# Two-layer hybrid backbone on one core: attention with one score buffer, z projections spread over its units, scan matmuls grouped by shape

## The chip, the core and the metric

The kernel runs on one core of a Trainium2 chip. The metric is device time in microseconds (us) of one execution. Five engines work beside each other, each taking its own instructions in order: TensorE (PE, matmuls, its weight loads shown apart as PEld), VectorE (DVE), ScalarE (ACT), GpSimd (POOL) and SyncE (SP, which issues most DMAs). Matmuls write to PSUM, which has eight banks of 512 fp32 columns.

## The reference, cut to what matters

Two layers work on 512 latent tokens and 256 context tokens of width 1024. Each layer is one mixer: normalise and modulate, one combined input projection, three head groups side by side, an output projection with a residual.

```
p = split_projection(h @ w_in)          # r,k,v,lora,z | conv b,c,h,z | q,k,v,z of the attention
rwkv:  S = S*w + (S a) b^T + v k^T ;  y = S r        (both directions, context first, then latents)
attn:  s = q k^T ;  p_j = softmax(s_j)  (j = 0, 1) ;  o = (p_0 - lam * p_1) v
       out = rms_norm(o) * silu(z)
x = x + gate * rms_norm(concat(rwkv, conv, attn) @ w_out)
```

The attention has four heads, each with two score maps. Layer 0 yields latents and context, so it has six query blocks of 128 rows; layer 1 yields latents only, four blocks.

## The kernel before, in words

Each operand of the big matmuls is split into a high and a low fp32r part, and a projection is three matmuls for each of eight 128-row slices (hi*hi, hi*lo, lo*hi). One projection of one 128-wide channel group is a run of 24 matmuls of 512 columns for the latents (`pcl`) and, where the context is needed, 24 of 256 columns (`pcc`); `proj_ch` is a Python generator that issues one of them per step. Token-major projections are `ptl` and `ptc`.

The projections not needed at once wait in a queue of generators, `fq`. `fill(us)` issues matmuls from the queue until their nominal lengths (0.213 us for 512 columns) sum to `us`; such filler stands between dependent steps. A list scheduler then orders each engine's instructions by priority, which is the place in the program, and by its own picture of when inputs are ready. `keep_in_program_order` pins an instruction behind the one issued before it on its engine; `T.matmul(..., tail=True)` does that and also raises its priority, so that a group of matmuls stays together.

A layer goes through these stages. First come the projections that the scan needs. Then the scan (`rwkv_scan`) runs in three blocks of four steps. A step works on both directions: `ch<-zu,R` (R0, state times stage matrix), a copy `gs` on DVE, `ch<-gs,XT`, four copies `zu` that alternate between ACT and DVE, `ch<-zu,R` again (R1), and four DVE additions that make the next `zu`. Where output is wanted there are also `yps<-zu,rt` (called rt below) and `yps<-zu,R` (R2). Every one of these is 8 fp32 matmuls, 16 instructions in the trace, on a part of the array: R0, R1 and R2 on 128x64, XT and rt on 64x64, while the filler uses 128x128. `fill(F["a"])`, `fill(F["b"])` and `fill(F["c"])` stand between them. In block 0 of layer 1 no output is wanted. Then `rwkv_out` normalises and transposes the scan's output, with filler beside it, and `fill(1e9)` empties the queue.

The attention (`attention`) is a software pipeline over units, a unit being one head and one query block (in layer 0 the two context blocks form one unit): 20 units in layer 0, 16 in layer 1. For a unit, PE writes the scores of both maps (`sc`, 8 matmuls) to a PSUM buffer of three banks, DVE takes two maxima (`mx`), ACT two exponentials (`e<-sc`), each with a read of the accumulator, DVE and POOL combine the maps, PE transposes (`aT_mm`, tile `aTp`), ACT copies (`aT_cp`), PE multiplies by v (`av`) and ACT drains the result with a copy and a square (`drain`, tiles `O`, `osq`). At iteration x the pipeline works on the scores of unit x+3, the exponentials of x+2, the combination of x+1 and the rest of x. `lin["on"]` pins all PE work of this stage in program order, and `order` does so for the main ACT and DVE work. `finish(h)` normalises a head, transposes it (`oT`), multiplies by silu(z) and writes the result, split, into slice 4+h of `lat` and `ctx`, which are the projections' own inputs.

Before the change the z projections of the attention (`z_gate`, four channel groups) are filler of the `rwkv_out` stage, and q and k of heads 2 and 3 (`qk(2)`, `qk(3)`) are filler of the attention's first three iterations (16 and three times 6 nominal us), with the rest issued at x = 0. Then the filler's three PSUM banks are given up (`az_done`), and a second score buffer `pr1` takes them: from there on the scores alternate between two buffers. The units themselves have no filler.

Of the kernel before, what the change touches and what calls it, by code (L numbers as in the profile page):

```python
# [50 lines left out]
EB = (3,2)  # L51
ATB = 2
ORD = [(0,), (4, 5), (1,), (2,), (3,)]
# [10 lines left out]
FI2 = 3  # L64
FA = (16,6)
QV = (2,3)
# [10 lines left out]
WM = 2  # L77
ZB = 1
PA = 3
# [27 lines left out]
def build(tc, A):  # L107
# [19 lines left out]
    class T:  # L127
        @staticmethod
        def matmul(*a, tail=False, **k):
            if tail:  # L130
                with tc.high_priority(offset=400):
                    tc.keep_in_program_order(nc.tensor.matmul(*a, **k))  # L132
                return
            i = nc.tensor.matmul(*a, **k)  # L134
            if lin["on"] or lin.get("next"):
                tc.keep_in_program_order(i)
                lin["next"] = False

        @staticmethod
# [674 lines left out]
    def rwkv_scan(l, st, rw, lat, cx):  # L814
# [38 lines left out]
        for b in range(3):  # L853
# [37 lines left out]
            for p in range(4):  # L891
# [15 lines left out]
                for d in range(2):  # L907
                    for hp, h, hr in HH:
                        T.matmul(pv[d][hr, 0, hp, :], R[d][:, hp, h, 0, :], zu[d][:, hp, h, :], start=True, stop=True)
                if want_y:  # L910
                    for d in range(2):
                        py[d] = ps("y", "yps").rearrange("p (k a v) -> p k a v", k=4, a=2)
                        for hp, h, hr in HH:
                            T.matmul(py[d][hr, 0, hp, :], prepd[d][0][hr, hp, cc[d][1], :], zu[d][hr, hp, h, :],
                                     start=(hp == 0), stop=False, tile_position=(h * 64, h * 64), skip_group_check=True)
                for d in range(2):
                    gs[d] = rw.tile([P, 2, HD], F32, tag="gs", bufs=2, name="gs")
                    V.tensor_copy(gs[d], pv[d][:, 0])
                if not end:
# [19 lines left out]
                if not end:  # L939
                    for d in range(2):  # L940
                        nz[d] = new_zu(nb, d, np_)
                        for hp, h, hr in HH:
                            T.matmul(pv[d][hr, 0, hp, :], R[d][:, hp, h, 1, :], zu[d][:, hp, h, :], start=True, stop=True)
# [110 lines left out]

    def z_gate(l, cnt, dst, mul, lat, cx, fk=()):
        last = l == L - 1
        n = NL if last else NT
        for h in range(cnt):
            t = fst("zs")
# [10 lines left out]
    def attn_proj(l, lat, cx):  # L1070
# [82 lines left out]
    def attention(l, lat, cx, pool, az_done, hd0):  # L1153
# [85 lines left out]
        def aT_mm(u, i):  # L1239
            b0, b1 = ((0, 3), (3, 6))[i] if len(u["tt"]) == 1 else ((0, 2), (2, 4))[i]  # L1240
            pt = u["pt"] = ps("a", "aTp")
            for kt in range(b0, b1):
                T.transpose(pt[:, (kt - b0) * P:(kt - b0 + 1) * P], u["e", 0][:, kt * P:(kt + 1) * P], ident)

        def aT_cp(u, i):
            b0, b1 = ((0, 3), (3, 6))[i] if len(u["tt"]) == 1 else ((0, 2), (2, 4))[i]
            if AC >> i & 1:
                dv(V.tensor_copy(u["aT"][:, b0 * P:b1 * P], u["pt"][:, :(b1 - b0) * P]))
            else:
                ac(S.copy(u["aT"][:, b0 * P:b1 * P], u["pt"][:, :(b1 - b0) * P]))  # L1250

# [24 lines left out]
        def finish(h, O):  # L1276
# [42 lines left out]
        def at(i):  # L1319
            return us[i] if 0 <= i < len(us) else None  # L1320

        for x in range(-3, len(us)):
# [10 lines left out]
            if p:  # L1333
                drain(p)
            if u:
                aT_cp(u, 0)
            if c:
                coef(c)
                combine(c)
            if e and x < 0:  # L1340
                expo(e, 0)
                expo(e, 1)
                e = None
            if w:
                scores(w, 0)
            if e:
                expo(e, 0)
            if u:
                aT_mm(u, 1)
                aT_cp(u, 1)  # L1350
            if w:
                scores(w, 1)
                maxi(w, 0)
                maxi(w, 1)
                head_next(w)
            if e:
                expo(e, 1)
            if u:
                av(u)
            else:  # L1360
                fill(FA[1])
            if u and u["i"] == FI and u["h"]:
                fins.append(finish(u["h"] - 1, Os[u["h"] - 1]))
                next(fins[-1])
            if u and u["i"] == FI2 and u["h"]:
                next(fins[-1])
        drain(us[-1])
# [78 lines left out]
    for l in range(L):  # L1446
# [23 lines left out]
        with tc.tile_pool(name=f"yy{l}", bufs=1, reuse_waits="tile") as yy:  # L1470
            with tc.tile_pool(name=f"rw{l}", bufs=1, reuse_waits="tile") as rw:
# [12 lines left out]
                ap1, ap2, az = attn_proj(l, lat, cx)  # L1484
                fq[:] = must + [rwkv_v(l, lat, cx), z_gate(l, 2, zrd[l], 0.5, lat, cx), conv(l, lat, cx)] + ap1
                rwkv_scan(l, st, rw, lat, cx)
# [30 lines left out]
            with tc.tile_pool(name=f"at{l}", bufs=1, reuse_waits="tile") as at:  # L1517
# [17 lines left out]
                if not YE:  # L1535
                    wo = y_split()
                psum_end(f"q0{l}", f"q3{l}")
                psum(f"y{l}", dict(b=3))
# [159 lines left out]
```

## Time and profile before

| | us |
|---|---|
| runs: lowest, median, highest | 1171.63, 1181.82, 1189.62 |
| the profiled execution's own time | 1183.87 |
| its span in the trace | 1181.6 |
| PE busy | 1061.3 |
| DVE busy | 733.6 |
| ACT busy | 525.2 |

A row of the timeline gives the start, the length, the engine, the line, the operation with out<-in, and the count of merged instructions; in brackets the engine's idle time before it and who ended that. Starts are us from the span's start. PE rows overlap: matmuls are pipelined, so the distance between starts is what a matmul costs. Line L134 and L118 are the helpers that record matmuls and DVE work. The granted clock (PEclk) is 1.00 at 2.4 GHz and 0.50 at 1.2 GHz.

### The profile page before, as it was taken

What the parts mean: (1) busy time and instruction counts of PE and PEld (TensorE: products, weight loads), DVE (VectorE), ACT (ScalarE), POOL (GpSimd) and SP (SyncE); (2) the same over time, 40 slices, a digit from 0 to 9 for tenths busy, and PEclk for the clock granted to TensorE, in tenths of its full rate; (3) what the DMA queues carried; (4) which work ended last, traced back from release to release, by engine and by line L of the source; (5) the groups of instructions that cost most, each with busy time, mean ns of one, the idle gap of its engine ahead of it and who ended that gap; (6) DMA issues with size and microseconds to landing.
All of it is one profiled execution on the core that took longest, in us unless ns stands there. A gap on an engine that the chain in (4) does not pass through costs nothing.

```text
span 1181.6 us, 25468 instructions
## 1 busy us (share of the span) xinstructions
PE 1061.3 (90%) x9850; PEld 857.7 (73%) x9850; DVE 733.6 (62%) x1712; ACT 525.2 (44%) x1330; POOL 485.6 (41%) x508
## 2 busy tenths in 40 slices
PE   4899989989699999979899899989969989988797
PEld 1577968667578867868777776866757876777675
DVE  3430658588647243389947867776893813569945
ACT  4323563353353223368733664655334422338731
POOL 1211524425624513355532345254572443456532
PEclk9999999999899999999999999999999989999999
DMA  9473321212424346745052452232331334555143
GB/s 350 169 238 116 89 78 47 60 28 70 144 55 117 122 148 203 205 153 139 14 183 72 143 178 78 85 92 59 95 99 50 104 101 128 181 153 176 46 151 107
DMA packets 92088, 142.55 MB, mean 121 GB/s; under 512 B 28192, under 2 KB 36416, under 8 KB 91968
## 3 DMA queue, kind: packets, MB, share of 16 engines
q1 hardware_dynamic: 88512, 136.14, 37.3%
q10 hardware_dynamic: 3456, 4.80, 1.2%
q8 instruction: 77, 1.26, 0.5%
q14 instruction: 43, 0.35, 0.1%
HBM read 110.99 MB, written 25.71 MB: 116 GB/s over the span
## 4 chain that ended last, share of the span: by engine, by line
PE 50%; DVE 22%; ACT 7%; issue 5%; DMA 5%; POOL 4%; SPq 1%; ACTq 0%; DVEq 0%; POOLq 0%
PE pcl L134 16%; PE op L134 6%; PE ptl L134 5%; PE pcc L134 4%; PE ch L134 3%; DVE mx L118 3%; PE yps L134 3%; PE ptc L134 3%; DVE bk L118 2%; DMA mraw<-in_mod_w_dram 2%; DVE rs_t L118 1%; PE av L134 1%; DVE qkr L118 1%; PE s L134 1%; DVE e L118 1%
## 5 line engine op out<-in xcount | busy, mean ns | idle before, releaser
L260 POOL TENSOR_TENSOR wlo<-wraw,whi 128x512 fp32r<-128x512 f32 x134 | 180.3, 1349 | 317.8 <-ACT whi L257 278.1
L134 PE MATMUL pcl<-lat,whi 128*128 128x512 f32 (+1 forms) x928 | 301.4, 399 | 3.5 <-issue 1.8
L134 PEld LDWEIGHTS pcl<-lat,whi 128*128 128x128 f32 x928 | 170.3, 190 | 43.7 <-issue 8.8
L134 PE MATMUL pcl<-lat,wlo 128*128 128x512 f32 (+1 forms) x464 | 185.8, 400 | 3.8 <-POOL wlo L260 3.8
L257 ACT CAST whi<-wraw 128x512 fp32r<-128x512 f32 x144 | 88.4, 618 | 170.8 <-DMA wraw<-in_w_in_dram 44.2
L134 PE MATMUL pcc<-ctx,whi 128*128 128x256 f32 x576 | 109.6, 287 | 2.3 <-DVE ctx L118 1.7
L134 PEld LDWEIGHTS pcl<-lat,wlo 128*128 128x128 f32 x464 | 88.3, 190 | 27.2 <-POOL wlo L260 5.7
L134 PEld LDWEIGHTS pcc<-ctx,whi 128*128 128x128 f32 x576 | 92.2, 191 | 8.7 <-issue 2.6
L134 PE MATMUL pcc<-ctx,wlo 128*128 128x256 f32 x288 | 83.1, 289 | 2.0 <-DVE wlo L118 2.0
L134 PE MATMUL ptl<-whi,lat 128*128 128x256 f32 x384 | 83.4, 300 | 0.0
L1215 ACT ACTIVATE e<-sc,mx 128x768 f32<-128x768 f32 (+1 forms) x80 | 66.5, 834 | 20.7 <-DVE mx L118 15.4
L118 DVE TENSOR_REDUCE mx<-sc 128x1 f32<-128x768 f32 (+1 forms) x72 | 63.6, 918 | 15.8 <-PE sc L134 15.8
L134 PE MATMUL av<-vA,aT 128*128 128x128 f32 x416 | 60.1, 288 | 14.9 <-ACT aT L1250 14.7
L134 PEld LDWEIGHTS av<-vA,aT 128*128 128x128 f32 x416 | 54.9, 197 | 21.9 <-ACT aT L1250 18.8
L134 PEld LDWEIGHTS ptl<-whi,lat 128*128 128x128 f32 x384 | 65.4, 200 | 2.7 <-issue 0.7
L924 POOL TENSOR_TENSOR pz<-zu,pc 64x128 f32<-64x128 f32 x88 | 37.4, 425 | 60.6 <-DVE zu L118 55.8
L118 DVE TENSOR_TENSOR R<-s,cs 128x384 f32<-128x384 f32 (+1 forms) x96 | 47.0, 529 | 23.8 <-PE s L132 23.2
L134 PE MATMUL sc<-KH,QS 128*128 128x256 f32 (+1 forms) x144 | 52.7, 379 | 6.1 <-ACT qkr L1083 3.2
L134 PE MATMUL ptl<-wlo,lat 128*128 128x256 f32 x192 | 58.1, 302 | 0.0
L134 PEld LDWEIGHTS pcc<-ctx,wlo 128*128 128x128 f32 x288 | 55.0, 191 | 4.0 <-DVE wlo L118 2.2
L118 DVE TENSOR_TENSOR qkr<-qkr,qks 128x512 f32<-128x512 f32 (+2 forms) x24 | 25.5, 1063 | 34.0 <-POOL qkr L1090 26.3
L134 PE MATMUL sc<-KL,QS 128*128 128x256 f32 (+1 forms) x144 | 46.2, 342 | 0.0
(441 smaller groups left out, 2447.0 us busy)
## 6 DMA issues: line engine op xcount, KB each, us to landing
wraw<-in_w_in_dram SPq DMA_DIRECT2D x144, 256.0 KB, 2.6
mraw<-in_mod_w_dram SPq DMA_DIRECT2D x96, 256.0 KB, 4.5
KH<-qd SPq DMA_DIRECT2D x32, 192.0 KB, 3.7
oraw<-in_w_out_dram SPq DMA_DIRECT2D x20, 256.0 KB, 4.1
qd<-qks SPq DMA_DIRECT2D x12, 384.0 KB, 2.4
qd<-qkr SPq DMA_DIRECT2D x12, 384.0 KB, 2.5
qks<-qkr SPq DMA_DIRECT2D x64, 64.0 KB, 2.2
zu<-vd SPq DMA_DIRECT2D x96, 32.0 KB, 2.1
```

Of the source, the lines that this page charges most:

```text
L118: i = f(*a, **k)
L134: i = nc.tensor.matmul(*a, **k)
L257: S.copy(hi, raw)
L260: eng.tensor_tensor(out=lo, in0=raw, in1=hi.bitcast(F32), op=ALU.subtract)
L924: G.tensor_tensor(out=pz[d][hr], in0=zu[d][hr, :, h, :], in1=prepd[d][1][hr, :, cc[d][1]].unsqueeze(2).to_broadcast([64, 2, HD]), op=ALU.mult)
L1215: ac(S.activation(ej[:, c], pb[:, c], AF.Exp, bias=mx[:, i:i + 1], accum_out=den[:, u["h"] * 6 + tt, j:j + 1]))
```

## The change

In the scan, the rt matmuls are issued after `fill(F["a"])`, right ahead of XT, and a scheduling edge keeps them behind the last `gs` copy. Within each group all matmuls but the first get `tail`; XT is pinned behind rt, and R2 behind R1.

In the attention, `qk(2)` and `qk(3)` become filler of the `rwkv_out` stage, and the z projections, now one generator for each head, become filler of the attention: 4 nominal us at its start and 3 in each of the first three iterations, then 1.1 (layer 0) or 0.8 (layer 1) in each unit, half behind each group of transposes. The filler's PSUM banks stay in use to the end, so there is one score buffer. The order in an iteration is now: exponential of map 0, drain, exponential of map 1, transposes with filler, their copies, combination, all scores, maxima, `av`. Since `finish` overwrites `lat`, its last part for heads 0 and 1 is put off to head 3, after all z projections. `zT` gets three buffers, `aT` one.

```diff
-ATB = 2
+ATB = 1
-FA = (16,6)
+FA = (4,3)
+FU = (1.1,0.8)
-ZB = 1
+ZB = 3
@@ rwkv_scan
-                        T.matmul(pv[d][hr, 0, hp, :], R[d][:, hp, h, 0, :], zu[d][:, hp, h, :], start=True, stop=True)
-                if want_y:
-                    for d in range(2):
-                        py[d] = ps("y", "yps").rearrange("p (k a v) -> p k a v", k=4, a=2)
...
+                        T.matmul(pv[d][hr, 0, hp, :], R[d][:, hp, h, 0, :], zu[d][:, hp, h, :], start=True, stop=True,
+                                 tail=d + hp + h > 0)
...
                 fill(F["a"] if want_y else F["n"])
                 adv(AS)
                 lin["next"] = MG & 8
+                if want_y:
+                    for d in range(2):
+                        py[d] = ps("y", "yps").rearrange("p (k a v) -> p k a v", k=4, a=2)
+                        for hp, h, hr in HH:
+                            i = T.matmul(py[d][hr, 0, hp, :], prepd[d][0][hr, hp, cc[d][1], :], zu[d][hr, hp, h, :],
+                                     start=(hp == 0), stop=False, tile_position=(h * 64, h * 64), skip_group_check=True,
+                                     tail=d + hp + h > 0)
+                            if i is not None:
+                                tc.add_manual_dep(i.ins, cp.ins.name, mybir.DependencyInfo(
+                                    mybir.DependencyClass.NoSync, mybir.DependencyReason.DATA), reason="order")
...
-                                 start=True, stop=True)
+                                 start=True, stop=True, tail=want_y or d + hp + h > 0)
...
-                                     start=False, stop=True, skip_group_check=True)
+                                     start=False, stop=True, skip_group_check=True, tail=not end or d + hp + h > 0)
@@ attn_proj
+        chs(l, [x + h for h in (2, 3) for x in (I_Q, I_KA)])
         chs(l, range(I_AZ, I_AZ + 4))
-        chs(l, [x + h for h in (2, 3) for x in (I_Q, I_KA)])
-        return [qk(0), v(0), qk(1), v(1)], [z_gate(l, 4, zd[l], sgc, lat, cx, FK2)], [qk(2), qk(3)]
+        return ([qk(0), v(0), qk(1), v(1)], [qk(2, FK2), qk(3, FK2)],
+                [z_gate(l, (h,), zd[l], sgc, lat, cx, FK2) for h in range(4)])
@@ attention
+            if h < 2:
+                yield
...
+        fu = FU[l]
...
-            if x == FX:
-                fill(1e9)
-                az_done()
...
+            if e:
+                expo(e, 0)
+            if p:
+                drain(p)
+            if e:
+                expo(e, 1)
             if u:
                 aT_mm(u, 0)
...
+                fill(fu * 0.5)
+                aT_mm(u, 1)
+                fill(fu * 0.5)
                 aT_cp(u, 0)
+                aT_cp(u, 1)
+            else:
+                fill(FA[1])
             if c:
                 coef(c)
                 combine(c)
...
             if w:
                 scores(w, 0)
...
                 scores(w, 1)
                 maxi(w, 0)
                 maxi(w, 1)
...
+            if u and u["h"] == 3 and u["i"] < 2:
+                fill(1e9)
+                fin_next(u["i"])
+        az_done()
@@ build
             def az_done():
                 psum_end(f"f{l}")
-                psum(f"q3{l}", dict(pr1=1), "right")
-                cur["pr"] = ["pr1", "pr0"]
```

## Rows read from the trace of the kernel before

**Rows 1.** Busy time by stretch: length, busy of PE, PEld, DVE, ACT, POOL, granted clock, DMA share, GB/s

```profile
405.00:434.00 29.00, 29.00 (x338) 19.38 (x334) 11.18 (x38) 5.27 (x15) 8.48 (x13) 1.00 0.36 101
541.00:593.00 52.00, 44.20 (x319) 38.80 (x319) 46.34 (x107) 41.83 (x136) 29.15 (x32) 1.00 0.25 63
```

**Rows 2.** Timeline of PE, one scan step of layer 0, from one XT to the next

```profile
405.50 0.68 PE L134 MATMUL ch<-gs,XT 64*64 64x64 f32 x16
...
408.96 0.69 PE L134 MATMUL ch<-zu,R 128*64 128x64 f32 x16
409.48 0.40 PE L134 MATMUL yps<-zu,R 128*64 128x64 f32 x6
...
413.16 0.33 PE L134 MATMUL ch<-gs,XT 64*64 64x64 f32 x4
```

**Rows 3.** Timeline of all engines, first attention unit of layer 0, with filler beside it

```profile
488.30 0.40 PE L134 MATMUL sc<-KH,QS 128*128 128x512 f32 x1
...
489.91 1.82 DVE L118 TENSOR_REDUCE mx<-sc 128x1 f32<-128x768 f32 x2 [3.05 <-PE sc L134]
...
490.17 0.62 PE L134 MATMUL pcl<-lat,whi 128*128 128x512 f32 x2
...
491.82 0.90 ACT L1215 ACTIVATE e<-sc,mx 128x768 f32<-128x768 f32 x1 [3.47 <-DVE mx L118]
...
493.50 0.20 ACT L1215 ACTIVATION_READ_ACCUMULATOR e<-sc,mx 128x1 f32 x1
493.58 0.61 PE L134 MATMUL pcl<-lat,whi 128*128 128x512 f32 x2
```

**Rows 4.** Timeline of PE and DVE, another scan step of layer 0: its chain of dependences

```profile
334.80 0.68 PE L134 MATMUL ch<-gs,XT 64*64 64x64 f32 x16
...
336.68 0.29 DVE L118 COPY zu<-ch 64x128 f32<-64x128 f32 x1 [0.45 <-ACT zu L935]
338.31 1.20 DVE L118 TENSOR_TENSOR zu<-pz,ch 64x128 f32<-64x128 f32 x4 [1.34 <-PE ch L134]
...
340.49 0.48 DVE L118 COPY gs<-ch 128x128 f32<-128x128 f32 x2
```

**Rows 5.** Timeline of ACT, layer 0: a drain, and the next instruction

```profile
562.39 0.27 ACT L1269 COPY O<-av 128x128 f32<-128x128 f32 x1
...
562.80 0.50 ACT L1250 COPY aT<-aTp 128x384 f32<-128x384 f32 x1
```

**Rows 6.** Timeline of PE, layer 0: first scores of heads 2 and 3, of the last unit

```profile
541.50 0.50 PE L134 MATMUL sc<-KH,QS 128*128 128x512 f32 x1
...
562.11 0.50 PE L134 MATMUL sc<-KH,QS 128*128 128x512 f32 x1
...
579.29 0.49 PE L134 MATMUL sc<-KH,QS 128*128 128x512 f32 x1
```

**Rows 7.** Timeline of PE: start of qk(2) and of the output projection, layers 0 and 1

```profile
470.69 0.63 PE L134 MATMUL pcl<-lat,whi 128*128 128x512 f32 x2
...
593.43 0.48 PE L134 MATMUL op<-wo00hi,ctx 128*128 128x512 f32 x1
...
1022.28 0.63 PE L134 MATMUL pcl<-lat,whi 128*128 128x512 f32 x2
...
1128.38 0.48 PE L134 MATMUL op<-wo00hi,lat 128*128 128x512 f32 x1
```

**Rows 8.** Timeline of PE, layer 0: second transposes of a finished head

```profile
551.14 0.55 PE L141 MATMUL oT<-ident,O 128*128 128x128 f32 x3 [0.58 <-ACT osq L1272]
```

**Rows 9.** Timeline of PE, third unit of layer 1, still with one score buffer

```profile
1055.74 0.80 PE L134 MATMUL sc<-KH,QS 128*128 128x512 f32 x1 [2.88 <-ACT e L1215]
...
1058.04 0.63 PE L134 MATMUL sc<-KL,QS 128*128 128x512 f32 x1
```

**Rows 10.** Busy time of that stretch, columns as in Rows 1

```profile
1055.34:1058.75 3.41, 3.01 (x10) 2.52 (x11) 0.04 (x1) 1.11 (x4) 0.73 (x1) 0.50 0.42 117
```

**Rows 11.** Timeline of PE, layer 0, first step of the scan's second block

```profile
318.22 1.12 PE L134 MATMUL ch<-gs,XT 64*64 64x64 f32 x16 [6.29 <-DVE gs L118]
```

More of the change, by code (lines that the diff above doesn't have):

```diff
@@ L137, in matmul @@
                 lin["next"] = False
+            return i
         @staticmethod
@@ L908, in rwkv_scan @@
                     for hp, h, hr in HH:
-                        T.matmul(pv[d][hr, 0, hp, :], R[d][:, hp, h, 0, :], zu[d][:, hp, h, :], start=True, stop=True)
-                if want_y:
-                    for d in range(2):
-                        py[d] = ps("y", "yps").rearrange("p (k a v) -> p k a v", k=4, a=2)
-                        for hp, h, hr in HH:
-                            T.matmul(py[d][hr, 0, hp, :], prepd[d][0][hr, hp, cc[d][1], :], zu[d][hr, hp, h, :],
-                                     start=(hp == 0), stop=False, tile_position=(h * 64, h * 64), skip_group_check=True)
+                        T.matmul(pv[d][hr, 0, hp, :], R[d][:, hp, h, 0, :], zu[d][:, hp, h, :], start=True, stop=True,
+                                 tail=d + hp + h > 0)
                 for d in range(2):
                     gs[d] = rw.tile([P, 2, HD], F32, tag="gs", bufs=2, name="gs")
-                    V.tensor_copy(gs[d], pv[d][:, 0])
+                    cp = V.tensor_copy(gs[d], pv[d][:, 0])
                 if not end:
@@ L942, in rwkv_scan @@
                         for hp, h, hr in HH:
-                            T.matmul(pv[d][hr, 0, hp, :], R[d][:, hp, h, 1, :], zu[d][:, hp, h, :], start=True, stop=True)
+                            T.matmul(pv[d][hr, 0, hp, :], R[d][:, hp, h, 1, :], zu[d][:, hp, h, :], start=True, stop=True,
+                                     tail=d + hp + h > 0)
                     for d in range(2):
@@ L1053, in conv, with z_gate @@
             nc.sync.dma_start(out=ycd[l][w, :, 0:n], in_=y[:, :n])
-    def z_gate(l, cnt, dst, mul, lat, cx, fk=()):
+    def z_gate(l, hs, dst, mul, lat, cx, fk=()):
         last = l == L - 1
         n = NL if last else NT
-        for h in range(cnt):
+        for h in hs:
             t = fst("zs")
@@ L1240, in aT_mm @@
             b0, b1 = ((0, 3), (3, 6))[i] if len(u["tt"]) == 1 else ((0, 2), (2, 4))[i]
-            pt = u["pt"] = ps("a", "aTp")
+            pt = u["pt", i] = ps("a", "aTp")
             for kt in range(b0, b1):
@@ L1247, in aT_cp @@
             if AC >> i & 1:
-                dv(V.tensor_copy(u["aT"][:, b0 * P:b1 * P], u["pt"][:, :(b1 - b0) * P]))
+                dv(V.tensor_copy(u["aT"][:, b0 * P:b1 * P], u["pt", i][:, :(b1 - b0) * P]))
             else:
-                ac(S.copy(u["aT"][:, b0 * P:b1 * P], u["pt"][:, :(b1 - b0) * P]))
+                ac(S.copy(u["aT"][:, b0 * P:b1 * P], u["pt", i][:, :(b1 - b0) * P]))
         def av(u):
@@ L1320, in at, with fin_next @@
             return us[i] if 0 <= i < len(us) else None
+        zg = list(fq)
+        def fin_next(h):
+            while any(g in fq for g in zg[:h + 1]):
+                fill(0.1)
+            if len(fins) <= h:
+                fins.append(finish(h, Os[h]))
+            next(fins[h])
+        fu = FU[l]
         for x in range(-3, len(us)):
@@ L1339, in attention @@
                 combine(c)
[L1340 to L1343, printed above, removed]
             if w:
                 scores(w, 0)
[L1346 to L1351, printed above, removed]
                 scores(w, 1)
@@ L1355, in attention @@
                 head_next(w)
-            if e:
-                expo(e, 1)
             if u:
                 av(u)
-            else:
-                fill(FA[1])
             if u and u["i"] == FI and u["h"]:
-                fins.append(finish(u["h"] - 1, Os[u["h"] - 1]))
-                next(fins[-1])
+                fin_next(u["h"] - 1)
             if u and u["i"] == FI2 and u["h"]:
-                next(fins[-1])
+                fin_next(u["h"] - 1)
+            if u and u["h"] == 3 and u["i"] < 2:
+                fill(1e9)
+                fin_next(u["i"])
+        az_done()
         drain(us[-1])
@@ L1484, in build @@
                 ap1, ap2, az = attn_proj(l, lat, cx)
-                fq[:] = must + [rwkv_v(l, lat, cx), z_gate(l, 2, zrd[l], 0.5, lat, cx), conv(l, lat, cx)] + ap1
+                fq[:] = must + [rwkv_v(l, lat, cx), z_gate(l, range(2), zrd[l], 0.5, lat, cx), conv(l, lat, cx)] + ap1
                 rwkv_scan(l, st, rw, lat, cx)
@@ L1536, in build @@
                     wo = y_split()
-                psum_end(f"q0{l}", f"q3{l}")
+                psum_end(f"q0{l}")
                 psum(f"y{l}", dict(b=3))
```

3 lines of the change are left out of this document (removed).

## The prediction

> **What bounds the kernel now.** I read the busy times by stretch first, because the change touches two stages with different limits. In the last scan block of layer 0 PE is busy 29.00 of 29.00 us, DVE 11.18 and ACT 5.27 [rows 1]: whatever PE loses there lengthens the kernel. In the attention's steady part it is the other way round: DVE is busy 46.34 of 52 us, and PE's 44.20 overstate it, since pipelined matmuls are counted to their ends [rows 1].
>
> Then I read PE's timeline of one scan step [rows 2]. From XT to XT it takes 7.66 us. Between the two lie 11 filler matmuls of 512 columns and the 80 narrow instructions of R0, rt, XT, R1 and R2, cut into eight runs; with the filler between them the shape changes 15 times. The reader should see that no row there has a wait in brackets: the time is PE's own.
>
> **The scan, sized.** Fifteen filler matmuls in a row, from 490.17 to 493.58, cost 3.41 us or 0.227 each [rows 3], so 11 cost 2.50. Sixteen narrow instructions followed by some of their own shape cost 0.52 us (408.96 to 409.48) or 0.0325 each [rows 2], so 80 cost 2.60. The rest, 2.56 us over 15 changes, makes 0.17 us a change. The new order has three narrow groups in a step (R0; rt with XT; R1 with R2), hence 6 changes or 1.02 us: 6.12 us, 1.54 less.
>
> The chain of dependences could be late next. XT ends at 335.48; the last `zu` copy ends at 336.97, 1.49 later; R1 takes 0.69, the additions 1.20, R0 0.69, `gs` 0.48 and XT 0.68 [rows 2, 4]. With 0.09 us at each of five hand-overs, as from the end of the maxima to the exponential [rows 3], that is 5.7 us. The rt group is now behind `gs` and ahead of XT, so up to 0.5 us of it is added: 6.2. PE and chain come out alike, so 1.5 us is what a step can give, and only where DVE and ACT are free. That holds in the last block of each layer: 6 stretches at 1.5 give 9.0. In the other blocks with output, DVE and ACT also prepare the next block (`adv`), and rt is moved past two such pieces; 6 stretches at 1.0, my choice between 0.5 and 1.5, give 6.0. Three stretches that end a block have 9 to 13 changes now and get 0.7 each, 2.1; five block ends get 0.4 each, 2.0. Block 0 of layer 1 has no rt and already 3 groups: nothing. Sum: 19 us saved. Bounds: nothing (chain and queued DVE work take it all) and 25 (1.54 in all 15 stretches and the ends).
>
> The pinning adds an order, not a wait on a semaphore. Queued behind a late `gs` are rt, XT and any tail matmul of the preparation; the filler is free in the scheduler's list, but on the chip it stands where it was put.
>
> **The attention, sized.** With one buffer the scores of a unit can't start before the last exponential of the unit ahead. The first unit of layer 0 shows that ring undisturbed, with filler on PE: scores from 488.30, maxima from 489.91, exponentials from 491.82, last read ending at 493.70 [rows 3]: 5.4 us. The exponentials start only after both maxima, and the maxima after all eight score matmuls. In the new order the drain, 0.41 us from its start to the next instruction [rows 5], lies between the two exponentials, so the ring is 5.8 us. A context unit has two thirds of the columns: I take 1.0 off, from a third of 1.6 for scores and of 1.8 for maxima. Now a unit takes 4.12 us: 20.61 us for five, from 541.50 to 562.11 [rows 6]. Against this stands that the warm-up loses its filler.
>
> Layer 0, from the start of qk(2), 470.69, to the output projection, 593.43: 122.7 us [rows 7]. New, from the same place (the two projections that change places have 96 matmuls of 512 and 96 of 256 columns each): 7 nominal us of z are 33 matmuls or 7.5 us; three rings without a drain 5.4 + 4.4 + 5.4 = 15.2; sixteen rings, 13 x 5.8 + 3 x 4.8 + 3 x 0.4 for the double drains = 91.0; from the last scores to the output projection 14.1 now [rows 6, 7], 13 when DVE is less full. Sum 126.7: 4.0 more.
>
> Layer 1, from 1022.28 to 1128.38: 106.1 us [rows 7]. New: 7.5 + 3 x 5.4 + 12 x 5.8 + 13 = 106.3: 0.2 more. But qk(2) and qk(3) there have 96 matmuls of 512 and 48 of 256 columns, the z projections only the 96: 48 x 0.12 = 5.7 us more ahead of the attention, of which I take 5, since PE waits a little in that stage.
>
> A finished head's second transposes wait for a drain (ACT `osq`) to free their PSUM buffer [rows 8]. That drain is now inside the ring, and behind the transposes stand two more groups with filler between them, together 2.5 us of PE (three groups of transposes at some 0.4, by 0.55 with the pipeline's end [rows 8], and twice three filler matmuls) against 0.94 us for an exponential, half of 1.88 [rows 3]: 1.5 us late with filler, 0.3 without, three of each over both layers, 5 us. Bounds: nothing (another buffer comes free first) and 9.
>
> Covered and costed at nothing: one `aT` buffer, because `av` of the unit ahead ends about 3 us before ACT's next copy (if not, 0.5 us a unit, a copy in [rows 5]); the z weights' loads, stores, casts and gates, which take free places of ACT, DVE, POOL and SP (an ACT instruction ahead of an exponential would cost about the 0.5 of a copy [rows 5] in its unit); the swaps and stores of qk(2) and qk(3) on SP's queue, now in the `rwkv_out` stage, where they can push the scan's normalisation on DVE. I take 0 for these, with bounds of 3 us gained and 6 lost. Attention: 4 + 5 + 5 = 14 us more. The ring's own doubt, 5.4 to 6.3 us, over 28 rings with a drain moves that by -11 to +14.
>
> **The sum.** -19 + 14 = -5 us: 1183.87 becomes 1178.9 for the profiled execution, which stands 2 us above the median of the runs; against the median 1181.82 I forecast **1177 us**.
>
> **Rivals.** *Slower: the clock.* In layer 1 the third unit still had one buffer. PE waited 2.88 us for the exponential [rows 9], the granted clock of that stretch was 0.50, the level of 1.2 GHz [rows 10], and the scores took from 1055.74 to 1058.67 [rows 9], 2.93 us where it was 1.6 [rows 3]. In the new loop PE waits in every ring, and longest once z is used up: 13.3 nominal us go at the start and 1.28 in a unit, so 30.7 last to the 14th unit of layer 0, and 20.4, at 0.85, to the 9th of layer 1; 14 units go without. Each ring at the lower level costs 1.33 us. In those 14 that is 19 us, 1196; in all 36 it is 48, 1225. From 22 rings on the change is slower by over 2%. Against it: in the steady part now, where PE also waits in each unit, the clock was 1.00 [rows 1].
>
> The Trainium skill's page TensorE: Matmul & The Clock Gate, section "A second HAM failure mode: psum-queue depth-cycling", says that PE idling briefly and often between groups that cycle through PSUM makes the clock swing and costs throughput. By that rule all 36 rings are in danger, 1225 us; the stretch at 1055.34 agrees with it at 0.50 [rows 10], the one at 541 doesn't at 1.00 [rows 1].
>
> *Faster: the waits for `gs` go too.* XT of the second block waits 6.29 us, because DVE has an addition for qk(0), itself waiting for POOL, queued ahead of the `gs` copy [rows 11]; layer 1 has a second wait of that kind. A new order on DVE may drop both, 12.6 us. With the scan's full 25 that is 1158, and with the transposes of the finished heads hidden 1153.
>
> *The grouping gives nothing:* queued DVE work holds the chain at 7 us or more, and only the attention's 14 are left: 1196.
>
> **How the numbers follow.** Forecast 0.52 (its own range 1164 to 1193), waits gone 0.20, clock 0.16, no gain from grouping 0.12. A measurement of this kernel can tell about 2%, 24 us, from no change, that is below 1158 or above 1205. Faster: most of the second case and a tail of the first, 0.20. Slower: over half of the clock's case and what the ring's doubt adds to the last, 0.17. The same: 0.63. The range takes in both rivals up to where a tenth is left on each side: 1152 to 1206.
>
> **What would show it.** Right: scan steps near 6.1 us with three narrow groups between filler runs; PE busy less than now in the same stretch; scores starting right after a read of the accumulator, every 5.8 us, with `pcl` in the first 14 units; DVE well below 46 of 52. Wrong: steps above 7 us with `gs` or `zu` waits in brackets (grouping), a granted clock of 0.50 in the units without filler (clock), rings above 6.3 us because ACT holds a cast or z gate ahead of the exponentials, or a PE wait in the `rwkv_out` stage that the moved qk projections bring.

## The result, and the profile after

The change made the kernel slower: a median of 1219.1 us (four runs, 1208.9 to 1221.2) against 1180.6 (1171.6 to 1189.6), a ratio of 1.0335 with a 95% interval of 1.0242 to 1.0428. The execution that was profiled took 1208.93 us, with a span of 1206.7 us in the trace; before, it took 1183.87, with a span of 1181.6. It is the shortest of its four (the others took 1217.7 to 1221.2), so the two traces show 25 of the 38.5 us that lie between the medians. Ratios and medians here and below leave out slow executions, in which the granted clock is lower over the whole run: of the attention part alone two of four (1266.5 and 1465.7 us).

First the windows that answer to [rows 1], same columns: the last scan block of layer 0, most of the attention of layer 0, the second half of that of layer 1.

```profile
389.00:408.00 19.00, 19.00 (x308) 15.31 (x309) 8.71 (x31) 3.58 (x10) 8.57 (x14) 1.00 0.41 121
470.00:551.00 81.00, 63.95 (x411) 55.24 (x411) 52.34 (x115) 47.50 (x143) 35.83 (x36) 0.96 0.47 135
...
1080.00:1154.00 74.00, 53.85 (x313) 44.73 (x313) 47.00 (x107) 34.56 (x102) 26.48 (x29) 0.86 0.18 51
```

The scan is still PE's own. In the attention no engine is near its limit any more: DVE is busy 52 of 81 us, where it was 46 of 52. That is what a ring of dependences, in which each engine waits for the one before, looks like.

PE's timeline of a scan step of that block, XT to XT, answers to [rows 2]:

```profile
395.74 0.63 PE L133 MATMUL ch<-gs,XT 64*64 64x64 f32 x16
...
398.03 0.57 PE L133 MATMUL ch<-zu,R 128*64 128x64 f32 x13
398.44 0.64 PE L133 MATMUL yps<-zu,R 128*64 128x64 f32 x16
...
400.24 0.57 PE L133 MATMUL ch<-zu,R 128*64 128x64 f32 x13
...
401.53 0.57 PE L133 MATMUL yps<-zu,rt 64*64 64x64 f32 x13
401.93 0.63 PE L133 MATMUL ch<-gs,XT 64*64 64x64 f32 x16
```

R1 runs into R2 and rt into XT: three narrow groups, 6 shape changes, 6.19 us where it was 7.66, with filler worth one 512-column matmul more.

All engines in one undisturbed unit of layer 1, from scores to scores, answer to [rows 3, 5, 6]:

```profile
1068.79 0.50 PE L135 MATMUL sc<-KH,QS 128*128 128x512 f32 x1
...
1070.49 1.82 DVE L119 TENSOR_REDUCE mx<-sc 128x1 f32<-128x768 f32 x2 [0.61 <-PE sc L135]
...
1072.41 0.90 ACT L1224 ACTIVATE e<-sc,mx 128x768 f32<-128x768 f32 x1 [2.38 <-DVE cf L119]
...
1073.30 0.26 ACT L1278 COPY O<-av 128x128 f32<-128x128 f32 x1
...
1073.71 0.91 ACT L1224 ACTIVATE e<-sc,mx 128x768 f32<-128x768 f32 x1
...
1074.49 0.22 ACT L1224 ACTIVATION_READ_ACCUMULATOR e<-sc,mx 128x1 f32 x1
...
1074.76 0.50 PE L135 MATMUL sc<-KH,QS 128*128 128x512 f32 x1
```

Each row waits for the one before: 1.70 us to the maxima, 1.92 to the exponentials, 2.35 to the next scores, 5.97 in all, where a unit took 4.12. The wait that ACT's first row puts down to `cf` is in the main the one for the maxima, which end at 1072.31; the small `cf` instruction ends 0.07 us behind them.

Three rows of PE answer to [rows 7, 11]: the wait of the second block's first XT, and the two output projections. The first came down from 6.29 to 5.18 us.

```profile
307.90 0.90 PE L133 MATMUL ch<-gs,XT 64*64 64x64 f32 x11 [5.18 <-DVE gs L119]
...
599.25 0.48 PE L135 MATMUL op<-wo00hi,ctx 128*128 128x512 f32 x1
...
1153.45 0.48 PE L135 MATMUL op<-wo00hi,lat 128*128 128x512 f32 x1
```

By stage (the scan from its first to its last `ch` matmul; "forecast" from the prediction's terms):

| change in us, both layers | forecast | trace |
|---|---|---|
| scans (213.4 to 194.9, 206.2 to 190.8) | -19 | -34 |
| scan's end to first scores (58.6 to 52.5, 38.6 to 36.8) | -15 | -8 |
| first scores to the last unit's scores (91.0 to 122.2, 73.4 to 107.7) | +33 | +65 |
| last unit's scores to the output projection (14.1 to 16.2, 15.3 to 17.5) | -3 | +4 |

The other stages differ by 3 us, ahead of the first scan. The third line is where the forecast went wrong: 34 rings took 230 us where it had 192 (4.4 to 5.8 a ring), and 5 more for late transposes.

Two stretches show what lengthens rings beside their own 5.97. In layer 1 the third scores start 15.69 us after the second. Rows of SP, ACT and PE:

```profile
1040.48 0.33 SPq L1102 DMA_DIRECT2D qd<-qks  x1
1041.99 0.33 SPq L1103 DMA_DIRECT2D qd<-qkr  x1
...
1043.35 1.11 SPq L252 DMA_DIRECT2D wraw<-in_w_in_dram  x2
...
1046.87 0.62 ACT L259 CAST whi<-wraw 128x512 fp32r<-128x512 f32 x1 [5.80 <-DMA wraw<-in_w_in_dram]
1047.54 1.22 PE L135 MATMUL pcl<-lat,whi 128*128 128x512 f32 x2 [9.10 <-ACT whi L259]
```

The weights of the z filler are loaded behind the stores of `qk(3)`, which SP can issue only when POOL, DVE and ACT are done with it. PE's order is written out, so the filler that waits for weights holds the scores behind it, though their buffer is free.

The other: DVE and PE at the end of a head in layer 1, and under it the window of the time behind (columns as above).

```profile
1108.56 0.88 DVE L119 TENSOR_TENSOR oss<-oss,r 128x4 f32<-128x4 f32 x2
...
1112.51 1.81 DVE L119 TENSOR_REDUCE mx<-sc 128x1 f32<-128x768 f32 x2
...
1115.89 0.90 PE L143 MATMUL aTp<-ident,e 128*128 128x128 f32 x3 [3.56 <-ACT osq L1281]
```

```profile
1114.39:1121.22 6.83, 5.33 (x20) 4.58 (x21) 3.02 (x8) 3.05 (x9) 2.75 (x3) 0.50 0.39 119
```

Between the first two rows stand 11 more instructions on 4 columns that normalise the finished head. The scores had been there since 1110.66, so the maximum is 1.8 us late; PE then waits 3.56, and the granted clock falls to 0.50.

### The profile page after: what moved, and what is told of

Same layout as the page of the kernel before. It is cut to its first block, busy times and chain, and to the rows that moved or that the text cites. A ratio compares the mean times of both kernels' runs of the same rounds, so it can differ in the third digit from the quotient of the medians.

```text
span 1206.7 us, 25490 instructions
## 1 busy us (share of the span) xinstructions
PE 1047.4 (87%) x9850; PEld 850.1 (70%) x9850; DVE 728.8 (60%) x1712; ACT 521.2 (43%) x1330; POOL 483.2 (40%) x508
## 3 DMA queue, kind: packets, MB, share of 16 engines
q8 instruction: 77, 1.26, 0.5%
## 4 chain that ended last, share of the span: by engine, by line
PE 37%; DVE 22%; ACT 8%; issue 6%; DMA 3%; POOL 3%; SPq 1%; DVEq 0%; ACTq 0%; POOLq 0%
PE pcl L135 8%; PE op L135 7%; DVE mx L119 5%; PE ptl L135 4%; PE sc L135 3%; ACT e L1224 2%; PE pcc L135 2%; PE ptc L135 2%; DVE bk L119 2%; PE ch L133 2%; DMA mraw<-in_mod_w_dram 1%; DVE rs_t L119 1%; PE aTp L143 1%; PE yps L133 1%; DVE Acc L119 1%
## 5 line engine op out<-in xcount | busy, mean ns | idle before, releaser
L135 PE MATMUL pcc<-ctx,whi 128*128 128x256 f32 x576 | 113.4, 292 | 2.0 <-DVE ctx L119 1.7
L143 PE MATMUL aTp<-ident,e 128*128 128x128 f32 x208 | 38.6, 297 | 46.0 <-ACT osq L1281 43.8
L1235 POOL TENSOR_TENSOR e<-e,cf 128x256 f32<-128x256 f32 x32 | 23.7, 740 | 109.1 <-DVE cf L119 79.3
L143 PEld LDWEIGHTS aTp<-ident,e 128*128 128x128 f32 x208 | 24.8, 148 | 57.7 <-ACT osq L1281 54.7
L135 PE MATMUL av<-vA,aT 128*128 128x128 f32 x416 | 57.4, 290 | 1.1 <-ACT aT L1259 1.1
```

Of the source, the lines that this page charges most:

```text
L143: i = nc.tensor.transpose(*a, **k)
L1235: G.tensor_tensor(out=e1, in0=e1, in1=cf[:, 0:1].to_broadcast([P, NC]), op=ALU.mult)
```

## The experiments

Kernels ran in five groups, each beside runs of the kernel before, whose median moved between 1179 and 1186; so the ratios to it are compared, and 0.01 is 11.8 us. By the intervals below, two ratios that lie less than some 0.006 to 0.016 apart (7 to 19 us), as their intervals are narrow or wide, can't be told from each other.

| | ratio to before | 95% interval | median us |
|---|---|---|---|
| the change | 1.0335 | 1.0242 to 1.0428 | 1219.1 |
| scan part alone | 0.9748 | 0.9678 to 0.9818 | 1147.9 |
| attention part alone | 1.0554 | 1.0427 to 1.0681 | 1244.1 |
| scan part, projections swapped | 0.9726 | 0.9671 to 0.9781 | 1150.2 |
| one buffer, old projections, no filler | 1.0433 | 1.0374 to 1.0491 | 1233.1 |
| the same, useless work | 1.0408 | 1.0345 to 1.0470 | 1230.1 |
| the change, z not spread | 1.0513 | 1.0452 to 1.0573 | 1241.2 |
| finish chain pinned | 1.0305 | 1.0244 to 1.0366 | 1214.5 |
| the same, useless work | 1.0255 | 1.0210 to 1.0300 | 1213.5 |
| drain first | 1.0239 | 1.0167 to 1.0310 | 1207.9 |
| z weights by ACT's queue | 1.0234 | 1.0186 to 1.0283 | 1210.3 |
| all four | 1.0120 | 1.0068 to 1.0172 | 1194.8 |
| all but the pin | 1.0068 | 1.0031 to 1.0104 | 1191.0 |
| two half buffers, pin | 0.9866 | 0.9807 to 0.9925 | 1167.4 |
| two half buffers, no pin | 0.9668 | 0.9608 to 0.9727 | 1145.8 |

**The two parts.** The scan's part of the diff on the kernel before, and the rest of the diff without it.

> The kernel before with the scan part of the change alone. Theory 1 (the trace after the change): both scans got shorter, 213.4 to 194.9 and 206.2 to 190.8 us, and what follows them takes as long as in the kernel before, so 34 us go: about 1147 us against the median of 1180.6. Theory 2 (the size of the prediction): 19 us, about 1162; the other 15 belong to the attention part or to where its filler went. Theory 3: the shorter scan only brings the wait for weights and for the normalisation forward, and the stage behind the scan gives most of it back: above 1170.

> The changed kernel with the scan's old order of matmuls, so the attention part alone. Theory 1 (the trace after the change): from the scan's end to the output projection layer 0 takes 27.1 us more and layer 1 34.7 us more, 62 in all: about 1242 us. Theory 2 (the size of the prediction): 14 us, about 1195; then the loss would come from the two parts meeting. If the two parts just add, this run and the scan-only run differ from the kernel before by amounts that sum to the whole change, +39 us.

The scan part takes 0.025 off, 30 us, near the trace's 34; the attention part adds 0.055, 65 us: theory 1 both times. They add up to 0.030 against the whole's 0.0335, so within the intervals neither part changes what the other is worth. The second kernel's interval is the widest, so its size is the less certain.

**Swap, buffer, spreading.** In the scan-only kernel the projections change places:

```diff
...
-        return [qk(0), v(0), qk(1), v(1)], [z_gate(l, 4, zd[l], sgc, lat, cx, FK2)], [qk(2), qk(3)]
+        return [qk(0), v(0), qk(1), v(1)], [qk(2, FK2), qk(3, FK2)], [z_gate(l, 4, zd[l], sgc, lat, cx, FK2)]
```

> The kernel with the scan part alone and two score buffers, where only the projections change places: q and k of heads 2 and 3 in the rwkv_out stage, z as filler ahead of the units. Theory 1: the swap has a price of its own, which the trace of the changed kernel shows as 4.0 and 3.1 us more than forecast ahead of the first scores, 3.3 for the first maxima behind the rotation of qk(3), and the wait for z weights: 10 to 18 us more than the scan part alone, 1158 to 1166. Theory 2: with two buffers and all z ahead of the units nothing waits for it: 1148 to 1152; then the price in the changed kernel comes from the swap together with the ring.

No price that the intervals show (0.9726 to 0.9748): theory 2. That the swap's waits cost only where a ring hangs on them fits this, but is argued. The next kernel is the changed one with `z_gate` and `qk` put back, `FA = (16,6)`, `FU = (0,0)` and `fill(1e9)` at x = 0:

> The changed kernel with one score buffer and the new order of the units, but with the projections where they were before: z in the rwkv_out stage, q and k of heads 2 and 3 as filler ahead of the units (16 and three times 6 nominal us, the rest at the first unit), no filler in the units. Theory 1 (the serial ring is the price): against the scan part alone, 1148, 32 units take 5.97 instead of 4.12 us, 59 more, 1207; all units are without filler now, and if a ring in two or three runs at the clock 0.50 that is 12 to 20 more: 1207 to 1227, about the changed kernel's 1219. Theory 2 (the moved projections are the price: the wait for z weights of 9 us, the late first maxima of 3, the later start of the units by 7): without them the ring alone gives 1180 to 1195.

One buffer, together with the order of the units that goes with it, costs 0.0685, 81 us, against the scan part alone, even with the projections in their old places: theory 1, and more than it said. In the traces the rings are 63 us longer together (224.2 us against 160.8), and the time from the scan's end to the first scores 12, where the new order has filler ahead of the scores. No kernel has the new order with two whole buffers, so the two aren't separated. Next, the changed kernel with `FU = (0,0)` and all z issued ahead of unit 0:

> The changed kernel with all z projections issued ahead of the first unit, none in the units. Theory 1 (filler in a ring is free, since the ring and not PE sets the pace): 18.5 us of PE work in layer 0 and 7.6 in layer 1 come out of the rings and stand ahead of them, so it is 26 us slower, and up to 15 more for rings at the clock 0.50, now that no unit has filler: 1245 to 1260. Theory 2 (the filler costs in the ring almost what it saves ahead of it: 0.2 to 0.3 us of late scores in a ring, ACT's and DVE's z work, the waits for weights): 1215 to 1230.

0.018 above the change, 21 us, between the two theories: most of the 26 us of PE work was hidden in the rings, though some 5 of the 21 come from scores at 0.50, in 12 rings here and in 6 after the change. Spreading does what it is for, and gives back a quarter of what the buffer costs.

**What lengthens the rings.** The drain ahead of the exponentials:

```diff
+            if p:
+                drain(p)
             if e:
                 expo(e, 0)
-            if p:
-                drain(p)
-            if e:
                 expo(e, 1)
```

> The changed kernel with the drain of a unit ahead of the exponential of map 0 instead of between the two. Theory 1 (the ring sets the pace): the ring of scores, maxima, exponentials, 5.97 us in an undisturbed unit, has the drain's 0.41 us in it; av ends 3.1 us after the scores start and the maxima 3.5, so the drain fits in front and all but 0.1 of it leaves the ring: 28 rings by 0.3 to 0.4 make 8 to 11 us less than the changed kernel. Theory 2 (PE sets the pace, with 1.66 us of scores, 0.9 of transposes, 1.5 of av and 1.1 of filler in a unit): no change in units with filler, 16 rings by 0.35 or some 5 us in those without. Theory 3: av is late in the units with filler, so that ACT holds the exponentials for it: slower by up to 0.5 us in 20 rings, 10 us.

ACT and PE rows of that kernel, the unit shown above:

```profile
1071.83 0.27 ACT L1278 COPY O<-av 128x128 f32<-128x128 f32 x1 [2.34 <-PE av L135]
...
1072.35 0.91 ACT L1224 ACTIVATE e<-sc,mx 128x768 f32<-128x768 f32 x1
...
1074.02 0.20 ACT L1224 ACTIVATION_READ_ACCUMULATOR e<-sc,mx 128x1 f32 x1
...
1074.27 0.50 PE L135 MATMUL sc<-KH,QS 128*128 128x512 f32 x1 [0.84 <-ACT e L1224]
```

The drain now runs while ACT would wait for the maxima; undisturbed rings take 5.48 us, with filler too, and all rings together 217.4 us where they took 229.9. The ratio falls by 0.0096, 11 us; the intervals overlap, but ratio and trace agree with theory 1, that the ring sets the pace. The weights:

```diff
-        pin(nc.sync.dma_start(out=raw, in_=src_ap), 8)
+        pin((S if lin["on"] and out_tag is None else nc.sync).dma_start(out=raw, in_=src_ap), 8)
```

> The changed kernel, but the weights of the z projections are loaded by ACT's DMA queue instead of SP's. Theory 1: PE's idle 9.1 us at 1047.54 in layer 1 is the price of the moved qk(2) and qk(3): the loads of the next z weights stand on SP's queue behind the stores of qk(3), which wait for its rotation on POOL, DVE and ACT (stores at 1040.48 and 1041.99, loads at 1043.35). Then that ring falls from 15.7 to some 6 us and the kernel by 9 to 10, to about 1209. Theory 2: the loads are not the point, the cast on ACT and the subtraction on POOL that make the weights are late as well: less than 4 us. Theory 3: ACT waits for a free weight buffer ahead of its exponentials: no gain or a loss.

The ring that took 15.69 us takes 6.81:

```profile
1042.66 0.79 PE L135 MATMUL sc<-KH,QS 128*128 128x512 f32 x1 [2.89 <-ACT e L1224]
...
1049.47 0.50 PE L135 MATMUL sc<-KH,QS 128*128 128x512 f32 x1 [0.35 <-ACT e L1224]
```

So theory 1 holds for this ring. For the kernel it is less sure: the ratio is 0.010 lower, 12 us, at the edge of what the intervals tell, and in the trace all rings together lose only 4.7 us (225.2), since others got longer; one rose from 9.13 to 10.75 us, its maximum 4.1 us late. The finish chain: each DVE instruction of `finish`, up to its first yield, goes through `dv`, which pins it behind the one before:

```diff
-                if lin["dve"]:
-                    tc.keep_in_program_order(i)
+                if lin.get("dv"):
+                    lin["dv"](i)
...
+            lin["dv"] = dv if h < 3 else None; V.reciprocal(r0[:, :ntt], d_)
...
+            y, lin["dv"] = zT, None
```

> The changed kernel; only the place of one chain on DVE is altered: the small instructions that normalise a finished head (reciprocal, r, rs, ors) are pinned behind the two maxima of their iteration, where the program writes them. Theory 1: in the changed kernel this chain stands ahead of a waiting maximum, holds it up by 2.5, 1.85 and 1.8 us in layer 1 and by 0.9, 0.7 and 0.3 us in layer 0, and the idle PE behind it then runs one ring at the clock 0.50, which costs 1.1 us more in four rings: some 12 us go, ratio to the changed kernel 0.99, and the windows at 0.50 near 1087, 1114 and 1142 go too. Theory 2: the windows at 0.50 come from the units without filler, whatever DVE does: they stay, and 8 us go at most. Theory 3: the chain only moves, and holds up the coefficients or the transposes of the finished head: no change.

Not told from no change (0.003). In layer 1 the maxima came on time, 1.70 us after the scores' start instead of 4.19 and 3.52, but five rings without filler, three of them in layer 1, now ran their scores in part or throughout at 0.50 (one in the changed kernel), in two the maximum was 1.3 us late behind the pinned chain, and in layer 0 two first maxima came 2.9 and 2.1 us late: theories 2 and 3 both in part. Then that kernel with 8 useless transposes in each unit without z, and the one-buffer kernel with them in every unit:

```diff
+        def keep(us):
+            if fq:
+                return fill(us)
+            pt = ps("f", "dum")
+            for k in range(4):
+                T.transpose(pt[:, k * P:(k + 1) * P], ident, ident)
...
-                fill(fu * 0.5)
+                keep(fu * 0.5)
...
```

> The kernel with the finish chain behind the maxima, and with 8 useless transposes of the identity in each unit that has no z filler left, where the filler stood. With the finish chain moved, every second or third ring of those units ran at the clock 0.50 (7.24 us against 5.97), some 9 rings in all. Theory 1 (the units without filler let the clock fall): all these rings come to 5.97, some 11 us less than that kernel's 1214.5, so about 1203. Theory 2 (the clock falls behind PE's single long waits of 1.7 to 2.7 us for the drain, which the useless work doesn't shorten): no change. Theory 3: the useless work stands in the scores' way, 0.9 us in 14 units: up to 12 us slower.

> The kernel with one score buffer, projections where they were before and no filler in the units (1233), with 8 useless transposes of the identity in every unit. Theory 1 (the clock is a cost of its own): its trace had 15 windows at 0.50 in the two attentions and some 13 rings that they lengthen by 0.5 to 1.3 us; they go, and the time falls by 10 to 16, to about 1220. Theory 2 (what the runs with the finish chain suggest, where the windows went and the median fell by 1): within 4 us of 1233. Theory 3: the useless work, 1 us in each unit, delays transposes and scores: slower.

The windows of both attentions in the one-buffer kernel, first without the useless work:

```profile
498.00:612.00 114.00, 81.97 (x456) 68.71 (x456) 66.56 (x149) 59.40 (x192) 41.01 (x44) 0.85 0.25 68
1058.00:1175.00 117.00, 78.66 (x432) 66.03 (x431) 72.53 (x146) 54.86 (x149) 45.35 (x48) 0.82 0.30 90
```

and with it:

```profile
498.00:608.00 110.00, 84.90 (x592) 75.47 (x591) 66.42 (x149) 58.57 (x190) 40.18 (x43) 0.94 0.25 69
1058.00:1170.00 112.00, 80.30 (x524) 71.39 (x525) 69.04 (x141) 54.25 (x151) 41.88 (x45) 0.88 0.29 86
```

The clock rises from 0.85 and 0.82 to 0.94 and 0.88, and the ratios fall by 0.0025 and, in the pinned kernel, 0.005: 3 and 6 us, both within what the runs can't tell from nothing. That doesn't make the clock cheap. Without the useless work 15 rings of this trace have scores at 0.50 for some or all of their time, which lengthens the scores by 0.35 to 1.26 us each, 14.6 in all; with it there are still 8 such rings, with 7.0 us. Half of the price went, yet all rings together fell only from 224.2 to 223.6 us, so the useless work takes about as much as it gives. What the clock alone costs is not isolated.

**What is left.** All four edits, then all but the pin:

> The changed kernel with all four: drain ahead of the exponentials, finish chain behind the maxima, z weights on ACT's queue, useless transposes in the units without filler. If the causes are separate they add: 5 for the chain, 11 for the drain, 10 for the loads, 11 for the clock, so 1219 becomes about 1182. What is left above the scan part alone (1148), some 34 us, is then the price of the ring itself, 5.5 us a unit against 4.12 with two buffers, and nothing accidental. If the mends share one slack, the sum is smaller and the time stays above 1195. If the ring is not what sets the pace, mending all this should come near 1150.

> The changed kernel with the drain ahead of the exponentials, z weights on ACT's queue and useless transposes in the units without filler, and the finish chain where the scheduler puts it. Theory 1: the pin cost as much in the rings of 5.5 us as it did with two half buffers, some of it: 1175 to 1190, below the 1194.8 with the pin. The ring of one whole buffer, 5.5 us against 4.1, in 32 units less the z work that it hides, leaves it 30 to 40 above the 1146 to 1148 of the scan part alone and of two half buffers. Theory 2: the chain costs the same wherever it stands in a ring as long as this: 1193 to 1200.

With all four 0.0215 goes, 25 us, where 37 were expected. Without the pin it is 1.0068, between the two theories, and the difference can't be told from nothing; that is still 0.032 or 38 us above the scan part alone. Its rings sum to 208 us in the trace, 44 more than in the kernel before. Undisturbed they take 5.49 us, 5.00 for context units, which over 34 rings is 185 us, 20 more than before; the other 24 lie mostly in 14 rings of 5.9 to 8.2 us, so the mends didn't end the disturbances. Last, the buffer in two tiles of two banks, one for each map, z's filler with two banks instead of three; the combination moves ahead of the transposes, the z weights stay on ACT's queue, and there is no useless work:

```diff
-            psum(f"q0{l}", dict(pr0=1))
+            psum_end(f"f{l}")
+            psum(f"q0{l}", dict(s0=1, s1=1))
+            psum(f"g{l}", dict(f=2), "right")
...
             if e:
                 expo(e, 0)
             if p:
                 drain(p)
             if e:
                 expo(e, 1)
             if c:
                 coef(c)
                 combine(c)
             if u:
                 aT_mm(u, 0)
             if w:
                 scores(w, 0)
                 maxi(w, 0)
...
```

> The changed kernel with the score buffer cut in two: two banks for each map, taken by giving the z filler two banks instead of three, so that the scores of map 0 can start when the first exponential has been read, while the second runs; finish chain and z weights as in the mended kernels, no useless work, drain between the exponentials. Theory 1 (the serial ring of one buffer is the price): no engine has more than 5.2 us of work in a unit with filler (PE) and 4.2 without, so rings fall from 5.97 to these, 45 to 60 us go, and the time is 1160 to 1175, though z is still spread over the units. Theory 2 (spreading z and its loads over the units is the price, or the clock): the time stays near that of the mended kernel, 1182 to 1200. Theory 3: it even beats the scan part alone, 1148, since the warm-up without units has become shorter by 10 nominal us of filler in layer 0.

> The kernel with the score buffer in two halves, without the pin on the finish chain (1167.4 with it). In that run's trace five rings, two in layer 0 and three in layer 1, take 7.0 to 9.7 us where the others take 3.4 to 5.3, with a first maximum 5.0 to 7.6 us behind the start of its scores: the pinned chain of small instructions stands ahead of it. Theory 1: the pin costs in these short rings what it saved in the long ones; without it these rings fall by 2 to 4 us each, some 12 us in all: 1155. It stays above the scan part alone, 1148, because the z projections lengthen the units that have them by PE's time. Theory 2: the chain holds up a maximum wherever it stands, since DVE has no free place for its 4 us: 1164 to 1170. Theory 3: below 1146, so that the changed attention with two half buffers is better than the old one.

In the first of the two, DVE and PE rows of a head's end in layer 0:

```profile
508.43 2.76 DVE L119 TENSOR_TENSOR oss<-oss,r 128x6 f32<-128x6 f32 x2
...
516.53 1.81 DVE L119 TENSOR_REDUCE mx<-sc 128x1 f32<-128x768 f32 x2
516.76 0.52 PE L143 MATMUL aTp<-ident,e 128*128 128x128 f32 x3 [2.81 <-DVE e L119]
```

The pinned chain stands ahead of a combination and two maxima; with the combination it is 8 us long. That kernel, at 1167.4 us, came out as theory 1 said. Without the pin another 0.020 goes, 23 us, to 1145.8, the edge of theory 3. The attention windows of that second kernel:

```profile
470.00:555.00 85.00, 77.98 (x535) 69.47 (x535) 73.22 (x151) 64.91 (x197) 44.66 (x46) 1.00 0.49 142
1010.00:1070.00 60.00, 52.73 (x344) 45.04 (x343) 55.86 (x113) 45.25 (x122) 36.88 (x40) 1.00 0.50 151
```

DVE is busy 56 of 60 us again, the clock is at 1.00 throughout, and the kernel, at 0.967, is faster than the kernel before and than the changed one; whether it also beats the scan part alone (0.975) the intervals leave open.

## Why the prediction was wrong

**The scan: right mechanism, term too small.** The last blocks' steps came to 5.99 to 6.19 us (6.12 forecast), and the 15 stretches from XT to XT within the blocks saved 18.9 (17.1 forecast). But 15 more went between the blocks, for which it had 2, and the upper bound of 25 failed with it: in the three transitions that got shorter PE waits 6.2 us less (1.1 of it for `gs`), and 3.4 us of next-block preparation (`s`) and 2.8 us of filler had moved into the shortened steps. The rival in which grouping gives nothing is out.

**"Faster: the waits for `gs` go too": no.** They stayed, at 5.18 and 6.85 us, where they were 6.29 and 6.87.

**The attention: +62 where 14 stood.** The ring was read rightly from [rows 3, 5]: 5.97 us undisturbed against 5.8, 5 us in all. What failed is the step that multiplied it by the units and added 5 us for one disturbance, with the z weights' loads and the stores of `qk` at nothing. In these rings, which have no slack, nearly every late instruction is paid. The excess of 38 us in the trace, ring by ring: 10 for the z weights (step "costed at nothing", bound 6 us, and it named the wrong victim: SP's queue held PE, not DVE); 10 for maxima that DVE had work ahead of, in the first ring the rotation of `qk(3)`, later the finish chain; 6 for scores at 0.50; 6 for filler and late transposes that ran past the last exponential; 5 to 6 for the ring itself. The mend of the weights confirms their 10 us for that ring, though not for all rings together; the drain's place, worth 11, was within the forecast's 5.8; the chain's share is not confirmed, since pinning it moved the wait. The late transposes, costed at 5 from [rows 8], made four waits of 0.7 to 1.4 us, 4.2 in all, but by the trace only one of them, 1.26 us, was for ACT's `osq` as the prediction had it; the other three were for DVE's `zT`. That this size came out was luck.

**Ahead and behind: 7 and 8 us more than forecast.** Before the first scores PE waits 1.2 us more in each layer; what makes the rest is open. Behind the last scores it was to be 1 to 2 us shorter, "when DVE is less full", and got longer: PE waits there 2.63 and 3.56 us for a drain (`osq`), in layer 1 behind a last maximum that the finish chain holds up by 1.8 us. No run isolates these.

**"Slower: the clock": the right side, a small part of the cause in the trace.** Its 1196 to 1225 us hold the measured 1219.1, but not by its own way. Windows at 0.50 came, at waits of PE of 1.9 to 9.1 us, and hit the scores of 6 rings, where 22 were needed: 6 of the 38 us. Useless work that halves the number of such rings brings 3 to 6 us at most, its own cost included. How much the clock adds to the median is open: the three runs of the change that weren't profiled took 9 to 12 us more than the profiled one, at a mean granted clock of 0.952 to 0.954 where that one had 0.960.

**"The same", then, failed by two errors of opposite sign:** in the traces the scan came out 15 us better and the attention 48 us worse than forecast, so a good part of the second error is hidden by the first.

## What to carry to other kernels

When a pipeline goes from two buffers to one, price the ring, then every queue that any of its members stands in: here nearly each instruction that was placed ahead of one of them, on any engine, was on the path. If banks are short, cut the buffer where its readers change (here between the two maps) before halving its depth: with two half buffers 1.0335 became 0.9668, which includes the weights' other queue, worth some 0.01 by itself, and the new order of a unit, which no run prices. Run the two halves of a change apart; here a gain of 30 us lay under a loss of 65.

## What the runs showed of the hardware

The size of a shape change held: 7.66 to 6.19 us, with 9 changes fewer and 0.227 us more filler, makes 0.19 us each if all of the difference is put down to them, where the prediction had 0.17.

Not expected: DVE instructions on 4 columns, 0.16 us each, grew to 1.26 and 0.76 where POOL had just begun one of its own. DVE and POOL, layer 1 after the change:

```profile
1082.13 1.27 POOL L345 TENSOR_TENSOR lat<-yc,lat 128x512 fp32r<-128x512 f32 x1 [1.11 <-DVE oss L119]
...
1082.16 1.26 DVE L119 TENSOR_SCALAR rs_i<-oss 128x4 int32<-128x4 int32 x1
...
1083.46 0.76 DVE L119 TENSOR_SCALAR rs_y<-rs_i 128x4 f32<-128x4 f32 x1
1083.46 1.52 POOL L1154 MEMSET KL<- 64x768 f32 x2
...
1084.26 0.16 DVE L119 TENSOR_TENSOR rs_t<-rs_y 128x4 f32<-128x4 f32 x1
```

In the unit shown further up, one such instruction of 1.12 us (at 1110.48) makes half of the 1.85 us by which the maximum came late. The traces of all 16 kernels bear the link out: of the 2080 DVE instructions of this chain on 4 or 6 columns, none of the 1816 that ran while POOL was idle took more than 0.18 us, and 162 of the 264 that ran beside a POOL instruction took 0.45 to 2.56 us. No run takes POOL's work away, so that POOL is the cause is not isolated.
